# An mLSTM stage taken two chunks at a time, with its 64-channel products in two halves of the array

## The chip, the cores and the metric

The kernel runs on one core of a Trainium2 chip. The metric is the device time of one execution in microseconds; three runs of the kernel before gave 2682.82, 2683.15 and 2689.93 us. The profile is of one more execution. Engines are named as in the profile: PE multiplies matrices (PEld is its weight load), DVE, ACT and POOL work on elements, and SP issues the transfers (DMA).

## What is computed

One layer of a bidirectional encoder, for 2048 tokens of 1024 numbers in float32: a norm, one large projection, a gated delta rule (GDN) in 8 heads, an mLSTM in 8 heads, an output projection, a norm and a residual. The change concerns the mLSTM alone. For one head and one direction it is, with C and n carried from chunk to chunk:

```python
m_t = jnp.maximum(b_c + m_state[..., None], mi_c)
inter = jnp.exp(b_c + m_state[..., None] - m_t)
w_intra = jnp.exp(lw_c - m_t[..., None]) * qk_c
num = inter[..., None] * jnp.einsum('bhld,bhde->bhle', q_c, c_state) + jnp.einsum('bhts,bhse->bhte', w_intra, v_c)
den = inter * jnp.einsum('bhld,bhd->bhl', q_c, n_state) + jnp.sum(w_intra, axis=-1)
h = num / jnp.maximum(jnp.abs(den), jnp.exp(-m_t))[..., None]
c_state = carry_dec[..., None, None] * c_state + jnp.einsum('bhld,bhle->bhde', wk, v_c)
```

q and k have 64 channels a head, v has 128. Both directions' h are added, normed over the head, and multiplied by two gates. The kernel works with chunks of 128 tokens, 16 a head, and appends a column of ones to v, so that den is column 128 of num.

## The kernel before

**Stages.** Norm, projection of gates, q, k, v of the GDN (to some 827 us of the span); then the rest of the projection beside the inversion of the GDN's triangular matrices, in which the mLSTM's q, k and v are made, convolved and stored to DRAM (827 to 1400 us: functions `m_k`, `m_q`, `m_v`, and `merges`); then the GDN's scan over chunks (1400 to 2063 us); then the mLSTM's chunks, with the first half of the output projection woven in as filling (2063 to 2476 us); then the rest of the output projection.

**The mLSTM stage.** Head by head, 16 chunks each, from the last chunk to the first. For each chunk `weights` makes scores k·q with one product over 128 rows (L1336; rows 64 to 127 of the weights are zeros that POOL set once, since there are only 64 channels), two exponentials on ACT (L1339) and one product on DVE (L1344: W). `core` then adds two products per direction in PSUM: scaled q times the state (L1382, the other direction's 64 rows being zeros) and W times v (L1386). DVE makes the denominators (L1389, L1390, L1393), ACT scales the first direction (L1395) and DVE adds the second (L1397), ACT sums the squares (L1402). Both directions' states lie in one tile of 128 rows, direction 0 in rows 0 to 63; `states` makes the sum k v for the next head, one step per chunk, with two accumulating products of 128 columns (L1274, the keys lying beside 64 zero columns), and DVE updates the state (L1282). POOL spreads the keys (L1229), masks the decay rows (L1320) and multiplies the decay by q (L1328: `qe`).

**What sets the order.** PE's and POOL's orders are written out by hand in this stage; `weave` puts 648 matmuls of the output projection (L1183, 128x512) evenly between the steps of `core`, two steps a chunk, 2.57 matmuls a step. DVE, ACT and SP follow an order that a scheduler chose when the kernel was built; every engine works through its own list in that order. In the stage from 827 to 1400 us PE alone is ordered by hand. PSUM in the mLSTM stage: 2 banks for scores, 2 for `pn` (one chunk each), 1 for the states, 1 for transposes, 2 for the filling.

In `m_q` the conv's result is stored to `mkq_d` and released. `load_block` loads scores' operands and decay rows two blocks of 4 chunks ahead.

## Time and profile before

| what | us |
|---|---|
| median of 3 runs | 2683.15 |
| profiled execution, own time | 2685.29 |
| its span, first to last instruction | 2683.6 |
| stage with the inversions and the mLSTM's q, k, v | 827 to 1400 |
| start of the mLSTM stage | 2063 to 2132 |
| mLSTM chunks with states woven in | 2132 to 2428 |
| mLSTM chunks without (the last head) | 2428 to 2470 |

Lines with an L are lines of the kernel before. A matmul in float32 over 128 or 129 columns shows as two records (two passes), one in the filling as one record. Starts of successive matmuls tell how long PE takes for one; the recorded length also holds the time until its last result is out, which overlaps the next.

### The profile page before, as it was taken

The page shows a single profiled execution, that of the slowest core. Times are in us where ns is not written, and L with a number is a line of the kernel's source. Part 1 is how long each engine was busy: PE and PEld are TensorE (multiplying, and loading weights), DVE is VectorE, ACT ScalarE, POOL GpSimd, SP SyncE. Part 2 cuts the span into 40 slices and gives each one's busy share as a digit, 9 for nine tenths or more (in the row PEclk, how much of TensorE's full clock was granted, in tenths as well). Part 3 has the DMA queues.
Part 4 walks back from the last instruction along what each step waited for, and adds up shares of the span by engine and source line. Part 5 has one row for each costly group of instructions (what it writes and reads, how often), then busy time and mean ns, then how long its engine had stood idle before and what let it go on. Part 6 is the DMA issues. An engine that isn't in the chain of part 4 may idle for free.

```text
span 2683.6 us, 49675 instructions
## 1 busy us (share of the span) xinstructions
PE 2575.4 (96%) x16974; PEld 2174.6 (81%) x16974; DVE 1652.3 (62%) x4062; ACT 1220.8 (45%) x3284; POOL 1010.3 (38%) x1497
## 2 busy tenths in 40 slices
PE   7999999999999999999999999999999699999998
PEld 6778877778887877778788888888888599998887
DVE  5547767777777888888625555555554466665333
ACT  6446666666662334344333333333333455555221
POOL 2136655676553333333211121212112455554133
PEclk9999999999999999999999999999998799999999
DMA  4135555565554344444436777667775888875564
GB/s 155 56 91 171 173 154 169 168 181 177 159 171 156 111 150 133 152 146 142 146 121 201 212 218 216 192 197 213 209 215 162 247 241 234 236 215 153 190 197 151
DMA packets 453158, 468.21 MB, mean 174 GB/s; under 512 B 34825, under 2 KB 306089, under 8 KB 452905
## 3 DMA queue, kind: packets, MB, share of 16 engines
q1 hardware_dynamic: 452905, 465.03, 57.9%
q8 instruction: 136, 2.23, 0.3%
q14 instruction: 117, 0.96, 0.1%
HBM read 301.92 MB, written 162.99 MB: 173 GB/s over the span
## 4 chain that ended last, share of the span: by engine, by line
PE 61%; DVE 12%; issue 10%; DMA 9%; POOL 5%; ACT 3%; SPq 1%; POOLq 0%; DVEq 0%; ACTq 0%
PE acc L273 33%; PE po L1183 5%; DVE cacc L586 3%; DMA E<-grow_d 2%; DVE tmp L843 2%; DVE dm L847 2%; PE ps L1017 2%; PE pn L1386 2%; PE pn L1382 2%; PE po L1054 2%; PE ps L1040 2%; PE po L1053 2%; PE ps L1008 2%; DMA wr<-in_w_in_dram 2%; PE pc L1274 2%
## 5 line engine op out<-in xcount | busy, mean ns | idle before, releaser
L273 PE MATMUL acc<-hh,wh 128*128 128x512 f32 x2048 | 832.7, 407 | 0.0
L273 PE MATMUL acc<-hl,wh 128*128 128x512 f32 x2048 | 826.5, 404 | 0.0
L273 PE MATMUL acc<-hh,wl 128*128 128x512 f32 x2048 | 821.7, 401 | 0.0
L273 PEld LDWEIGHTS acc<-hh,wl 128*128 128x128 f32 x2048 | 388.1, 189 | 72.5 <-issue 1.0
L273 PEld LDWEIGHTS acc<-hh,wh 128*128 128x128 f32 x2048 | 388.3, 190 | 69.7 <-issue 1.2
L273 PEld LDWEIGHTS acc<-hl,wh 128*128 128x128 f32 x2048 | 388.5, 190 | 69.1 <-issue 1.0
L231 POOL TENSOR_TENSOR wl<-wr,wh 128x256 fp32r<-128x256 f32 x256 | 205.2, 815 | 605.0 <-ACT wh L230 453.9
L586 DVE SCALAR_TENSOR_TENSOR cacc<-raw,gcw,cacc 128x512 f32<-128x512 f32 x256 | 214.7, 866 | 77.9 <-POOL raw L602 38.8
L1183 PE MATMUL po<-woh,ch 128*128 128x512 f32 x512 | 210.8, 412 | 12.7 <-ACT woh L1159 11.9
L1183 PE MATMUL po<-wol,ch 128*128 128x512 f32 x512 | 207.5, 406 | 2.3 <-POOL wol L1160 2.3
L1183 PE MATMUL po<-woh,cl 128*128 128x512 f32 x512 | 206.5, 404 | 0.0
L151 POOL TENSOR_TENSOR rs<-rs,mhalf 128x4 f32<-128x4 f32 x64 | 64.1, 1008 | 367.0 <-DVE rs L148 222.4
L230 ACT CAST wh<-wr 128x256 fp32r<-128x256 f32 (+1 forms) x260 | 97.8, 403 | 221.6 <-DMA wr<-in_w_in_dram 138.6
L717 POOL COPY dg<-T 32x128 f32<-32x128 f32 x256 | 151.1, 590 | 16.6 <-DVE T L707 6.7
L707 DVE SCALAR_TENSOR_TENSOR T<-pk,sc,E 128x256 f32<-128x256 f32 x256 | 109.7, 474 | 47.4 <-PE pk L704 39.6
L893 POOL COPY Z<-ZD 32x256 f32<-32x256 f32 x128 | 91.7, 717 | 114.3 <-DMA Z<-uq_d 77.9
L586 DVE SCALAR_TENSOR_TENSOR cacc<-raw,mcw,cacc 128x512 f32<-128x512 f32 x128 | 101.0, 807 | 41.2 <-ACT cacc L582 20.8
L586 DVE SCALAR_TENSOR_TENSOR kq<-raw,gcw,kq 128x512 f32<-128x512 f32 x128 | 102.5, 806 | 31.9 <-ACT kq L582 22.1
L1183 PEld LDWEIGHTS po<-woh,ch 128*128 128x128 f32 x512 | 97.5, 191 | 26.9 <-ACT woh L1159 12.6
L1183 PEld LDWEIGHTS po<-wol,ch 128*128 128x128 f32 x512 | 97.4, 190 | 16.8 <-POOL wol L1160 3.8
L1045 DVE SCALAR_TENSOR_TENSOR sn<-sn,eGL,ps 128x128 f32<-128x128 f32 x224 | 67.9, 345 | 69.7 <-PE ps L1040 69.7
L1183 PEld LDWEIGHTS po<-woh,cl 128*128 128x128 f32 x512 | 97.2, 190 | 14.6
(604 smaller groups left out, 4973.2 us busy)
## 6 DMA issues: line engine op xcount, KB each, us to landing
kv<-kv_d SPq DMA_DIRECT2D x256, 256.0 KB, 3.7
wr<-in_w_in_dram SPq DMA_DIRECT2D x256, 128.0 KB, 2.7
uq_d<-T SPq DMA_DIRECT2D x64, 512.0 KB, 4.0
uq<-uq_d SPq DMA_DIRECT2D x256, 128.0 KB, 3.6
zg_d<-zt SPq DMA_DIRECT2D x64, 256.0 KB, 2.7
E<-grow_d SPq DMA_DIRECT2D x64, 256.0 KB, 6.0
kv_d<-tk SPq DMA_DIRECT2D x64, 256.0 KB, 2.5
Z<-uq_d SPq DMA_DIRECT2D x32, 512.0 KB, 4.4
```

The source lines that it names most:

```text
L151: nc.gpsimd.tensor_tensor(out=rs, in0=rs, in1=mhalf[:, :CB], op=ALU.pow)
L230: nc.scalar.copy(out=hi, in_=raw[:, :, :n])
L231: nc.gpsimd.tensor_tensor(out=lo, in0=raw[:, :, :n], in1=hi.bitcast(F32), op=ALU.subtract)
L273: nc.tensor.matmul(ps, l[:, k % KH, :], r[b][:, k, :], start=(k == 0 and i == 0), stop=(k == KC - 1 and i == 2),)
L586: nc.vector.scalar_tensor_tensor(out=acc, in0=raw[:, t : t + TB], scalar=cw[:, t * n_ct + ct : t * n_ct + ct + 1], in1=acc, op0=ALU.mult, ...
L707: nc.vector.scalar_tensor_tensor(out=T2[d][:, :, i], in0=pk, scalar=sc[:, u, c : c + 1], in1=E[d][:, i].unsqueeze(1).broadcast_to([P, 2, P ...
L717: nc.gpsimd.tensor_copy(out=dg[qs, :, at : at + CB], in_=T2[d][qs, 1, :, qs].rearrange("p c i -> p i c"),)
L843: nc.vector.tensor_tensor(out=tv, in0=L[:, j, j + 1 : 32].unsqueeze(2).broadcast_to([P, n, m_]), in1=M[:, j : j + 1, 0:m_].broadcast_to([P ...
L847: nc.vector.tensor_tensor(out=M[:, j + 1 : 32, 0:m_], in0=M[:, j + 1 : 32, 0:m_], in1=tv, op=ALU.subtract,)
L893: nc.gpsimd.tensor_copy(out=self.Z[bs, :, :, bs], in_=ZD[bs].rearrange("p x (d c) -> p d c x", d=2)[:, :, self.qs],)
L1045: nc.vector.scalar_tensor_tensor(out=sn[d], in0=st[d], scalar=eGL[:, u, c : c + 1], in1=ps[d][:, 2], op0=ALU.mult, op1=ALU.add,)
L1183: nc.tensor.matmul(po, l[:, i, :], r[:, ns], start=(first and i == 0 and j == 0), stop=(last and i == H - 1 and j == 2),)
```

## The change

- `m_q` (second stage): for each of 16 blocks of 512 tokens and each direction, two loads of the decay row `in_d`, spread over 64 partitions each, one POOL product over 128x512 with the conv's result, and two stores to new DRAM tiles `mqe_d`. `load_block` then loads the finished `qe` with one transfer; its POOL products (L1328), and the zeros in `qe`, `kq` and `wk` with the copies that spread the keys (L1229), go.
- `core` goes by pairs of chunks, four steps a pair. Both chunks' scores (64 rows each) run in the two row halves of the array, as do the two directions' products of scaled q and state; the states' products run in its two column halves. Number of matmul records is the same for these; W times v stays as it was.
- One PSUM tile `pn` of 4 banks holds a pair's four sums and, beside them, the next pair's scores. There is one such tile (`bufs=1`). The denominators are made for a pair at once. `ps_c` holds two states.

```diff
-            ps_q = st_.enter_context(tc.tile_pool(name="ps_q", bufs=2, space=PSUM, reuse_waits="tile"))
-            ps_n = st_.enter_context(tc.tile_pool(name="ps_n", bufs=2, space=PSUM, reuse_waits="tile"))
+            ps_n = st_.enter_context(tc.tile_pool(name="ps_n", bufs=1, space=PSUM, reuse_waits="tile"))
...
+                for d in range(2):
+                    t = mpool.tile([P, TB], F32, tag="tk", name="qs")
+                    for j in range(2):
+                        nc.sync.dma_start(
+                            out=t[j * 64 : (j + 1) * 64, :],
+                            in_=in_d[d * H + 2 * i + j, bs].partition_broadcast(64),
+                        )
+                    nc.gpsimd.tensor_tensor(out=t, in0=t, in1=so, op=ALU.mult)
+                    for j in range(2):
+                        nc.sync.dma_start(
+                            out=mqe_d[2 * i + j][d * 64 : (d + 1) * 64, bs],
+                            in_=t[j * 64 : (j + 1) * 64, :],
+                        )
...
+                            nc.tensor.matmul(
+                                pc[half(d), e], wks[h, b][:, i, d, :], vs[h, b][:, i, :],
+                                start=True, stop=True,
+                            )
...
+            def scores(pn, h, c):
+
+                kq, i = blk[h, c // CB][0], c % CB // 2
+                for d in range(2):
+                    nc.tensor.matmul(
+                        pn[:, d, 0, VW : VW + P], kq[half(d), i, 0, :], kq[half(d), i, 1, :],
+                        start=True, stop=True,
+                    )
...
+                    qe, pn = blk[h, b][1], pair_tile()
+                    if g + 1 < len(items):
+                        hn, cn = items[g + 1]
+                        scores(pn, hn, cn)
+                    for e in range(2):
+                        ce = c - 1 + e
+                        i = ce % CB
+                        for d, slot in enumerate((ce, NC - 1 - ce)):
+                            nc.tensor.matmul(
+                                pn[:, d, e, :VW], qe[half(d), i * P : (i + 1) * P],
+                                C[half(d), slot, :], start=True, stop=False,
+                            )
...
+                    for e in range(2):
+                        v = vs[h, b][:, (c - 1 + e) % CB, :]
+                        for d in range(2):
+                            nc.tensor.matmul(pn[:, d, e, :VW], W[e][:, d], v, start=False, stop=True)
+                    yield
+                    dn = ms.tile([P, 2, 2], F32, tag="dn", name="dn")
+                    den = pn[:, :, :, P]
...
+                    for e in (1, 0):
...
+                        nc.scalar.activation(
+                            out=oc, in_=pn[:, 0, e, :P], func=AF.Copy, scale=dn[:, 0, e : e + 1]
+                        )
+                        nc.vector.scalar_tensor_tensor(
+                            out=oc, in0=pn[:, 1, e, :P], scalar=dn[:, 1, e : e + 1], in1=oc,
+                            op0=ALU.mult, op1=ALU.add,
+                        )
```

**PE, one chunk in the loop before** (names: `pn` sums, `pq` scores, `pc` states, `pt` transposes of finished blocks, `po` filling):

```order
L1382 MATMUL pn<-C_22810,qe_22802 128x129
L1386 MATMUL pn<-v,W 128x129
L1382 MATMUL pn<-C_22810,qe_22802 128x129
L1386 MATMUL pn<-v,W 128x129
L1183 MATMUL po<-woh_22998,cl 128x512
L1183 MATMUL po<-woh_23008,ch 128x512
L1183 MATMUL po<-wol_23009,ch 128x512
L1336 MATMUL pq<-kq_22794 128x128
L1274 MATMUL pc<-v,wk_22772 128x129
L1274 MATMUL pc<-v,wk_22771 128x129
```

PE, one pair of chunks in the loop now, from the scores of the next pair to the first filling behind W times v:

```order
L1331 MATMUL pn<-kq 128x128 x2
L1381 MATMUL pn<-C_22984,qe 128x129 x4
L1269 MATMUL pc<-v,wk 64x129 x4
L1197 MATMUL po<-woh_23150,ch 128x512
L1197 MATMUL po<-wol_23151,ch 128x512
L1397 MATMUL pn<-v,W 128x129 x4
L1197 MATMUL po<-woh_23150,cl 128x512
```

Six half-array products over rows, four over columns and four full ones stand together, and the next row of L1331 comes behind some 8 fillings; it is the first writer of the one `pn` tile.

**ACT in the loop before** (`o` scales a chunk, `junk` sums its squares, `E` are exponentials):

```order
L1395 ACTIVATE o<-pn,dn 128x128
L1339 ACTIVATE E<-rb,cb 128x128 x2
L1402 ACTIVATE junk,so<-o 128x128
L1395 ACTIVATE o<-pn,dn 128x128
L1339 ACTIVATE E<-rb,cb 128x128 x2
L1402 ACTIVATE junk,so<-o 128x128
```

ACT in the loop now, one pair and a bit (`ch` and `acc` belong to the filling):

```order
L1341 ACTIVATE E<-rb,cb 128x128 x4
L1414 ACTIVATE o<-pn,dn 128x128
L1422 ACTIVATE junk,so<-o 128x128
L1414 ACTIVATE o<-pn,dn 128x128
L1422 ACTIVATE junk,so<-o 128x128
L1341 ACTIVATE E<-rb,cb 128x128 x4
L1414 ACTIVATE o<-pn,dn 128x128
L1185 CAST ch<-ct 128x1024
L1214 COPY acc<-po 128x512
L1422 ACTIVATE junk,so<-o 128x128
```

The exponentials no longer stand between a chunk's `o` and `junk`; the second `o` of a pair stands behind the first `junk`, and in some pairs the filling's `ch` or `acc` stands between them too.

**SP in the second stage now**, at the end of one `m_q` (before, the rows with `qs` were not there):

```order
L783 DMA mqe_d_113<-qs 64x512
L777 DMA qs<-in_d 64x512 x4
L901 DMA Z<-uq_d_69 128x2x512
L213 DMA wr<-in_w_in_dram 128x2x128 x2
L770 DMA mkq_d_107<-cacc 128x4x128 x2
L783 DMA mqe_d_113<-qs 64x512
L783 DMA mqe_d_114<-qs 64x512
L783 DMA mqe_d_113<-qs 64x512
L783 DMA mqe_d_114<-qs 64x512
L777 DMA qs<-in_d 64x512 x4
L960 DMA uq_d_68<-Z 256x1x512
```

A store of `qs` waits for its POOL product, and the loads behind it for the store; the weights' loads (`wr`) and the inversion's (`Z`) stand in the same queue.

## Rows read from the trace of the kernel before

**Rows 1.** The page: engines' busy time, share of the span, instructions.
```profile
PE 2575.4 (96%) x16974; PEld 2174.6 (81%) x16974; DVE 1652.3 (62%) x4062; ACT 1220.8 (45%) x3284; POOL 1010.3 (38%) x1497
```

**Rows 2.** Windows: length, then busy us by engine; clock, DMA share, GB/s.
```profile
core 0: us, PE busy (x) PEld busy (x) DVE busy (x) ACT busy (x) POOL busy (x), PEclk, DMA share, GB/s
827.00:1400.00 573.00, 545.70 (x5646) 438.49 (x5645) 425.10 (x839) 216.94 (x516) 173.35 (x302) 0.98 0.43 137
2063.00:2132.45 69.45, 40.49 (x174) 35.06 (x174) 26.21 (x67) 21.88 (x53) 23.17 (x24) 0.68 0.89 251
2132.45:2435.02 302.57, 302.54 (x2120) 277.42 (x2121) 187.66 (x698) 165.63 (x570) 172.21 (x187) 1.00 0.82 230
```

**Rows 3.** Windows of line L1382 alone, four records a chunk.
```profile
2132.70:2428.00 295.30, 80.19 (x416) 68.81 (x417) 1.00 0.83 232
2428.00:2470.40 42.40, 13.96 (x72) 11.70 (x72) 1.00 0.45 132
```

**Rows 4.** Timeline of one chunk, all engines: start, us, what [idle before].
```profile
2156.09 0.39 PE L1382 MATMUL pn<-C,qe 128*128 128x129 f32 x2
...
2156.32 0.39 PE L1386 MATMUL pn<-v,W 128*128 128x129 f32 x2
...
2156.74 0.16 DVE L1389 TENSOR_TENSOR dn<-pn,em 128x2 f32<-128x2 f32 x1 [0.97 <-PE pn L1386]
...
2157.39 0.37 ACT L1395 ACTIVATE o<-pn,dn 128x128 f32<-128x128 f32 x1 [1.19 <-PE pq L1336]
2157.46 0.40 PE L1183 MATMUL po<-wol,ch 128*128 128x512 f32 x1
...
2157.69 0.39 PE L1183 MATMUL po<-woh,cl 128*128 128x512 f32 x1
...
2157.79 0.35 DVE L1397 SCALAR_TENSOR_TENSOR o<-pn,dn,o 128x128 f32<-128x128 f32 x1 [0.50 <-ACT o L1395]
2157.92 0.60 PE L161 MATMUL pt<-ident,o 128*128 128x128 f32 x4
2158.18 0.31 ACT L1402 ACTIVATE junk<-o 128x128 f32<-128x128 f32 x1 [0.42 <-DVE o L1397]
...
2158.36 0.39 PE L1382 MATMUL pn<-C,qe 128*128 128x129 f32 x2
...
2158.49 0.68 ACT L1339 ACTIVATE E<-rb,cb 128x128 f32<-128x128 f32 x2
```

**Rows 5.** Timeline of PE in the second stage, at products of 64 rows and columns.
```profile
1002.75 0.39 PE L273 MATMUL acc<-hl,wh 128*128 128x512 f32 x1
1002.98 0.39 PE L273 MATMUL acc<-hh,wl 128*128 128x512 f32 x1
1003.29 0.68 PE L877 MATMUL px<-Z,V 64*64 64x64 f32 x16
...
1004.18 0.44 PE L877 MATMUL p__10442<-VV,Z 32*32 32x32 f32 x15
1004.55 0.50 PE L273 MATMUL acc<-hh,wh 128*128 128x512 f32 x1
1004.88 0.39 PE L273 MATMUL acc<-hl,wh 128*128 128x512 f32 x1
```

**Rows 6.** Groups by form, PE, 827 to 1400 us: count, busy, mean ns, idle before.
```profile
L877 PE MATMUL px<-Z,V 64*64 64x64 f32 x512 | 22.2, 227 | 0.0
```

**Rows 7.** Groups by form, 2200 to 2400 us: count, busy, mean ns, idle before.
```profile
L1328 POOL TENSOR_TENSOR qe<-qe,kq 64x512 f32<-64x512 f32 x36 | 48.7, 1352 | 1.4
L1172 DVE TENSOR_TENSOR cl<-ct,ch 128x1024 fp32r<-128x1024 f32 x8 | 10.8, 1353 | 0.3
L1171 ACT CAST ch<-ct 128x1024 fp32r<-128x1024 f32 x8 | 8.3, 1039 | 1.3 <-PE po L1183 1.2
```

**Rows 8.** Transfers: KB each, median us from issue to landing.
```profile
mwk_d<-tk SPq DMA_DIRECT2D x32, 256.0 KB, 2.8
qe<-in_d SPq DMA_DIRECT2D x64, 128.0 KB, 4.3
kq<-mkq_d SPq DMA_DIRECT2D x32, 128.0 KB, 5.4
```

**Rows 9.** Waits from 827 to 1400 us: total, times, longest.
```profile
SPq L212 <- POOL wl L231: 81.0, 42, 7.5
PE pt L611 <- ACT cacc L591: 18.5, 5, 5.6
```

More of the change, by code (lines that the diff above doesn't have):

```diff
@@ L68 @@
     mkq_d = [dram.tile([2, 64, NC, 2, P], F32, name=f"mkq_d{i}") for i in range(H // 2)]
+    mqe_d = [dram.tile([P, S], F32, name=f"mqe_d{h}") for h in range(H)]
     mwk_d = [dram.tile([P, NC, 2, 64], F32, name=f"mwk_d{h}") for h in range(H)]
@@ L1249, with half @@
                 nc.vector.memset(C[:, 0, :], 0.0)
+            def half(d):
+                return slice(d * 64, (d + 1) * 64)
             def states(h):
                 C = Cs[h % 2]
-                if h == 0:
-                    spread_keys(0, outer)
-                    spread_keys(0, inner)
-                for t in range(NC):
+                first = pair_tile() if h == 0 else None
+                for t in range(0, NC, 2):
                     if h > 0 and t == 0:
                         load_values(h, inner)
-                        spread_keys(h, inner)
                     if h + 1 < H and t == NC // 2:
@@ L1305, in load_block @@
                     rb.append(t)
-                qe = qes[j % 3]
-                for d in range(2):
-                    nc.sync.dma_start(
-                        out=qe[d * 64 : (d + 1) * 64, d, :],
-                        in_=in_d[d * H + h, bs].partition_broadcast(64),
-                    )
+                qe = ms.tile([P, TB], F32, tag="qe", name="qe", bufs=3)
+                nc.sync.dma_start(out=qe, in_=mqe_d[h][:, bs])
                 blk[h, b] = (kq, qe, rb)
@@ L1317, in mask_block @@
                     return
-                kq, qe, rb = blk[h, b]
+                rb = blk[h, b][2]
                 for d in range(2):
@@ L1350, in core @@
             def core():
-                items = [(h, NC - 1 - i) for h in range(H) for i in range(NC)]
+                items = [(h, NC - 1 - i) for h in range(H) for i in range(0, NC, 2)]
                 ready = []
@@ L1355, in core @@
                 load_block(1)
-                for i, _ in enumerate(states(0)):
-                    if i % 2:
-                        yield
+                for _ in states(0):
+                    yield
                 mask_block(0)
-                nxt = weights(*items[0])
-                for k, (h, c) in enumerate(items):
+                pn = pair_tile()
+                scores(pn, *items[0])
+                h, c = items[0]
+                nxt = [weights(pn, h, c - 1 + e) for e in range(2)]
+                for g, (h, c) in enumerate(items):
                     C, W, b = Cs[h % 2], nxt, c // CB
@@ L1395, in core @@
-                    nc.scalar.activation(out=oc, in_=pn[:, 0, :P], func=AF.Copy, scale=dn[:, 0:1])
-                    next(following, None)
-                    nc.vector.scalar_tensor_tensor(
-                        out=oc, in0=pn[:, 1, :P], scalar=dn[:, 1:2], in1=oc,
-                        op0=ALU.mult, op1=ALU.add,
-                    )
-                    junk = ms.tile([P, P], F32, tag="junk", name="junk", bufs=1)
-                    nc.scalar.activation(
-                        out=junk, in_=oc, func=AF.Square, accum_out=so[:, i : i + 1]
-                    )
```

133 lines of the change are left out of this document (57 added, 76 removed).

## Prediction

> **What bounds the kernel now.** I read the shares first, then the stages, then one chunk. PE is busy for 96% of the span [rows 1], and in the mLSTM loop for 302.54 of 302.57 us at full clock [rows 2]: there the sum of PE's work is the time, and DVE, ACT and POOL (188, 166 and 172 us busy) lie beside it. The loop's pace: 416 records of L1382, four a chunk, in 295.30 us, so 104 chunks of 2.84 us, or 5.68 us a pair; the last 18 chunks, whose steps hold no states, take 42.40 us, 4.71 us a pair [rows 3]. In the stage's first 69 us PE idles 29 us while transfers move 251 GB/s; in the second stage it idles 27 of 573 us [rows 2].
>
> **One pair on PE, by parts.** A product of 129 columns is two passes; starts of L1382 and L1386 are 0.23 apart [rows 4], so I take 0.22 us a product. A filling takes 0.23 (2157.46 to 2157.69), four transposes 0.44 (2157.92 to 2158.36) [rows 4]. A pair before: 14 products, 3.1 us, 10.3 fillings, 2.36, and a block's transposes every second pair, 0.22 on average: 5.68, as measured. So the price list closes.
>
> **What the halves save.** Scores, q times state, and states are 10 of the 14 products. If two halves run side by side, they take the time of 5: 1.1 us a pair saved, 69 us over 64 pairs. That two run at once is seen for products of 64 rows and 64 columns: 16 passes in 0.68 us [rows 5]; taking off the 0.23 us that one record of this size lasts [rows 6], 0.45 us for 15 starts is 0.03 each, where 64 columns at the loop's rate (0.11 x 64/129) would be 0.055 alone. Those share neither rows nor columns. Halves that share all rows (states) or all columns (scores, q times state) don't occur in this trace; I take the full saving and keep none as the other end.
>
> **What it adds on PE.** Going from full products to halves, the first start is 0.31 behind the last full one instead of 0.23 (1002.98 to 1003.29), and the 15 starts lose some 0.05; going back costs about 0.09 before 1004.55 and 0.10 behind it (0.33 to the next instead of 0.23) [rows 5]. A pair crosses three times: full to row halves, row to column halves, back: 0.14 + 0.14 + 0.19 = 0.47 us. Bounds 0 and 0.6. PE's own work per pair is then 2.0 + 0.47 + 2.36 + 0.22 = 5.05 us.
>
> **The new wait.** There is one `pn` tile. The first product of a pair's first step (the next pair's scores) must wait until DVE's last add of the pair before has read it. Queued behind it on PE is everything: q times state, states, the fillings. Before, two tiles alternated and a chunk's reading had a whole chunk of PE work to hide in. So I add up the ring.
>
> Front, from the release to the last pass of W times v: three side-by-side products 0.67, states 0.45, crossings 0.47, 2.57 fillings 0.59, seven pass starts of W times v at 0.11, 0.78: 2.96 us.
>
> Back, from that last pass to the release, by a chunk in which nothing else stood between [rows 4]: the pass starts at 2156.43 (2156.32 and 0.11), ends 0.28 later, the denominators start at 2156.74, ACT's `o` at 2157.39, DVE's add at 2157.79, `junk` at 2158.18: 1.75 us. For a pair the three denominator steps come once. The second `o` stands behind the first `junk` on ACT, in the order now built: `junk` with its read-out holds ACT 0.31 (2158.18 to 2158.49), `o` 0.37, 0.03 to DVE, add 0.35, 0.04 to PE. Sum 2.85 us. PE has the fillings of three steps, 7.7 x 0.23 = 1.77, and every second pair the transposes, to cover it: 1.9 to 2.3 us with the last pass. The cover falls short by 0.6 to 0.95 us.
>
> Insertions: each 48 fillings, 4.7 pairs, bring one `ch` of 1.04 on ACT and one `cl` of 1.35 us on DVE [rows 7], and in the order built most of them stand inside the ring (`ch` between two `o`, or ahead of the exponentials; `cl` between the denominators or the two adds). Part of each falls into a gap; I take 1.6 of 2.4 us, 0.35 a pair, and 0.06 for the block's product with the gate between the two adds. Bounds 0 and 0.5.
>
> Ring: 2.96 + 2.85 + 0.41 = 6.2 us a pair, above PE's 5.05 and above the old 5.68. 52 pairs with states: +0.52 each, +27 us. Nine without: ring 6.2 less states and a crossing, 5.6, against 4.71: +8 us. Bounds of the two together: crossings and insertions zero -16, all at the upper end +50.
>
> The Trainium skill ("TensorEngine Tiling (Array Packing)", Performance Considerations, PSUM Bottleneck) says that tiling speeds up TensorE but not the emptying of PSUM, which may then become the bottleneck. By PE's 5.05 us alone the loop would gain 35 us, by the emptying it loses 35; the emptying's rows are those above.
>
> **m_q.** It gains 128 transfers and 32 POOL products. POOL's product over 64x512 took 1.35 us [rows 7]; 32 x 1.35 = 43 us, on an engine busy 173 of 573 us. A decay load of 128 KB lands in 4.3 us, a store in about 2.8 [rows 8]. With two `qs` tiles, a block's loads wait for the last block's stores, so a ring of some 4.3 + 2.7 + 2.8 and 8 issues holds each block for 13 us; blocks come every 7 us, the last two of each `m_q` at once. Behind these waits in SP's queue stand `wr` and `Z` loads, and the conv's buffer, two in all, is held longer, so ACT may wait to evacuate the next projection. Three PSUM banks (some 16 us of PE) and a weight column ahead cover most. SP waits for POOL 81 us there already, and PE lost 18.5 us at conv results [rows 9]. I take 2 us for each of 4 `m_q`: +8, bounds 0 and 40.
>
> **What it takes away elsewhere.** POOL's 64 products of `qe`, the key spreading and the masks' neighbours lie beside a full PE: nothing. In the stage's first 69 us, transfers set the pace; 128 KB a block less to load (the doubled `kq` half [rows 8]) for two blocks at 251 GB/s is 1 us, and first states no longer wait for spread keys: -2, bounds -5 and +3.
>
> **Sum.** +35 + 8 - 2 = +41 us. The profiled execution's 2685.29 (span 2683.6 and 1.7 around it) lies 2.1 above the median of the runs; 2683.15 + 41 gives **2724 us**.
>
> **Rivals.** *The fillings cover the emptying* (faster). Against: 2.85 against at most 2.3 us. For: every price in the ring that no row shows, crossings and insertions, could vanish. Then 5.34 a pair: 52 x -0.34 and 9 x +0.19, with m_q free and the start's 2 us, -18: 2665 us; PE alone (5.05) would be the floor, 2654. It decides at a ring of 5.6 us, 0.6 below mine.
>
> *The ring lands on the old pace* (no change): one of crossings and insertions vanishes, 5.75 us, m_q is free: +2 to +8 us, 2675 to 2691; centre 2685.
>
> *The halves don't run side by side* (the change doesn't do what it says): if the states run one after the other, +0.45 a pair, 52 pairs, +23: 2747 us; if the row halves do too, +0.67 for 61 pairs, +41: 2788. For: no row here shows halves that share rows or columns; against: rows 5's pairs. The Trainium skill ("TensorE: Matmul & The Clock Gate", Part 3: Packing small matmuls) says that a weight load overlaps a running matmul only if its row group differs; by that rule the states, which share all rows, would be the serial ones.
>
> *m_q stalls the second stage*: each conv buffer is released a ring (13 us) late, twice in four heads' pairs, and PE's 16 us of PSUM fall short by some 10 each: +40 in place of +8: 2756 us.
>
> **How the numbers follow.** Chances: forecast 0.50 (2692 to 2745), covered 0.12, old pace 0.13, serial halves 0.13 (half of it at 2747), m_q 0.12. A measurement here can tell 0.3%, 8 us, from no change. Faster 0.12, same 0.13, slower 0.75. The range reaches from the old pace's lower end, 2675, to just short of both halves serial, 2785; left out are the covered case and the dearest of the serial ones, 0.18.
>
> **What would show it.** PE busy well below 100% in the loop, its idle time at the scores (L1331) and ended by DVE's add (L1417); 6.2 us from one pair's first product to the next; ACT's `o` ended by DVE. Half products starting in twos within some 0.01 us, with 0.11 between twos, show the halves; 0.09 more at crossings the crossings. `pn` released before PE asks, and PE full, would make the forecast wrong, and so would SP or ACT waits on `qs` above 20 us.

## The result and the profile after

The changed kernel takes 2780.02 us (median of four runs, 2769.63 to 2783.64) against 2684.05 us: ratio 1.0347, 95% interval 1.0314 to 1.0379. The forecast was 2724 us, so the sign is right and the loss is more than twice as large. The profiled execution took 2782.27 us with a span of 2780.5. Lines with an L are now lines of the changed kernel: scores L1331, q times state L1381, states L1269, W times v L1397, fillings L1197; on ACT the exponentials L1341, `o` L1414, `junk` L1422, `ch` L1185, `acc` L1214; on DVE W L1346, denominators L1401, L1404, L1407, the adds L1417, `cl` L1186; POOL's masks L1316.

The two spans differ by 96.9 us. First records of a line divide it:

| stretch | before | after | difference |
|---|---|---|---|
| up to the scan's first product of w and uq | 1412.4 | 1437.9 | +25.5 |
| from there to the first states' product | 650.5 | 655.8 | +5.3 |
| start of the mLSTM stage, to its sixth pair | 81.2 | 75.4 | -5.8 |
| 50 pairs from there | 284.0 | 340.8 | +56.8 |
| the rest of the mLSTM pairs | 42.1 | 56.0 | +13.9 |
| the rest | 213.4 | 214.7 | +1.3 |

Shares first, against [rows 1]: PE has lost three points, with the same number of instructions.

```profile
PE 2584.2 (93%) x16974; PEld 2130.2 (77%) x16974; DVE 1645.6 (59%) x3870; ACT 1217.9 (44%) x3284; POOL 949.2 (34%) x1420
```

Windows of the changed kernel, in the columns of [rows 2]: second stage, 50 pairs.

```profile
827.00:1437.50 610.50, 569.71 (x5695) 456.38 (x5694) 442.76 (x842) 221.11 (x523) 222.68 (x335) 0.95 0.52 161
2169.00:2509.70 340.70, 279.21 (x1990) 221.57 (x1990) 158.67 (x505) 153.34 (x533) 80.69 (x100) 0.93 0.60 182
```

In the 50 pairs PE is busy for 279 of 341 us and its mean clock is 0.93, where it was full at 1.00. The same stretch by groups of PE (count, busy, mean ns, idle before and what ended it) has all of that idle time at one line:

```profile
L1331 PE MATMUL pn<-kq 64*128 64x128 f32 x200 | 26.1, 333 | 61.1 <-issue 44.6 <-DVE o L1417 16.4
```

So 61 us are waits at the scores, as forecast. They are for the tile, also where the profile names no releaser ("issue"): in 49 of the 50 pairs the scores start 0.10 to 0.15 us behind the end of DVE's second add, in one 0.30. A pair takes 6.82 us on average, where 6.2 was forecast. Here is one with nothing but the ring in the way, 6.02 us, from the timeline:

```profile
2223.90 0.49 PE L1331 MATMUL pn<-kq 64*128 64x128 f32 x4 [1.59 <-issue]
...
2224.77 0.66 PE L1269 MATMUL pc<-v,wk 128*64 128x129 f32 x8
2224.88 0.75 DVE L1346 SCALAR_TENSOR_TENSOR W<-E,pn 128x256 f32<-128x256 f32 x2 [1.08 <-PE pn L1381]
...
2226.16 1.05 PE L1397 MATMUL pn<-v,W 128*128 128x129 f32 x8
...
2227.25 0.16 DVE L1401 TENSOR_TENSOR dn<-pn,em 128x4 f32<-128x4 f32 x1 [0.97 <-PE pn L1397]
...
2227.91 0.37 ACT L1414 ACTIVATE o<-pn,dn 128x128 f32<-128x128 f32 x1 [1.30 <-DVE dn L1407]
...
2228.32 0.35 DVE L1417 SCALAR_TENSOR_TENSOR o<-pn,dn,o 128x128 f32<-128x128 f32 x1 [0.50 <-ACT o L1414]
...
2228.70 0.31 ACT L1422 ACTIVATE junk<-o 128x128 f32<-128x128 f32 x1 [0.42 <-DVE o L1417]
...
2229.01 0.35 ACT L1414 ACTIVATE o<-pn,dn 128x128 f32<-128x128 f32 x1
2229.43 0.34 DVE L1417 SCALAR_TENSOR_TENSOR o<-pn,dn,o 128x128 f32<-128x128 f32 x1
...
2229.92 0.49 PE L1331 MATMUL pn<-kq 64*128 64x128 f32 x4 [0.67 <-DVE o L1417]
```

This is the ring of the prediction, link by link: the second `o` behind the first `junk`, the next scores 0.15 us behind the end of the second add. Its sum without insertions was put at 5.81 us; eight pairs of this kind take 6.02 to 6.06. Two more take 5.83: they are the last step of a head, with four records of the states in place of eight. The 5.83 us that the expectations below name are theirs.

And here is a pair with insertions, 7.28 us, and the first products of the next one:

```profile
2298.01 0.49 PE L1331 MATMUL pn<-kq 64*128 64x128 f32 x4 [0.67 <-DVE o L1417]
...
2300.46 1.05 ACT L1185 CAST ch<-ct 128x1024 fp32r<-128x1024 f32 x1 [2.16 <-PE po L1197]
...
2301.65 1.39 DVE L1186 TENSOR_TENSOR cl<-ct,ch 128x1024 fp32r<-128x1024 f32 x1
...
2302.01 0.57 ACT L1214 COPY acc<-po 128x512 f32<-128x512 f32 x1
...
2302.48 0.69 ACT L1341 ACTIVATE E<-rb,cb 128x128 f32<-128x128 f32 x2
...
2302.96 0.15 DVE L1404 SCALAR_TENSOR_TENSOR dn<-pn,dn 128x4 f32<-128x4 f32 x1
...
2303.36 0.37 ACT L1414 ACTIVATE o<-pn,dn 128x128 f32<-128x128 f32 x1 [0.19 <-DVE dn L1407]
...
2305.29 0.79 PE L1331 MATMUL pn<-kq 64*128 64x128 f32 x4 [2.35 <-issue]
...
2306.87 1.13 PE L1269 MATMUL pc<-v,wk 128*64 128x129 f32 x8
...
2307.93 0.80 PE L1197 MATMUL po<-woh,ch 128*128 128x512 f32 x1
```

Between W times v and `o` stand `cl` on DVE, between the first and second denominators, and `ch`, `acc` and four exponentials on ACT. DVE's chain with `cl` ends last here: `o` waits 0.19 us for it. In other pairs it is the exponentials that end last. They wait for POOL's mask of the block, and `o` stands behind them, as in the pair that begins at 2188.29, where the denominators are ready at 2191.98:

```profile
2191.89 1.28 ACT L1341 ACTIVATE E<-rb,cb 128x128 f32<-128x128 f32 x4 [3.11 <-POOL rb L1316]
...
2193.08 0.35 ACT L1414 ACTIVATE o<-pn,dn 128x128 f32<-128x128 f32 x1
```

ACT's waits for that mask over the 50 pairs, in the kernel before, then in the changed one:

```profile
ACT E L1339 <- POOL rb L1320: 7.7, 17, 1.2
```

```profile
ACT E L1341 <- POOL rb L1316: 65.3, 21, 3.1
```

Behind the wait of 2.35 us the granted clock is at the lower of its two levels, 1.2 in place of 2.4 GHz (0.50 in the window below), and the next pair's products are longer: scores 0.79 us in place of 0.49, a first filling 0.80 in place of 0.50. Behind the wait of 0.67 us at 2298.01 the clock is 1.00 and they are not longer.

```profile
2305.40:2308.00 2.60, 2.60 (x21) 2.04 (x21) 0.75 (x2) 0.79 (x4) 0.00 (x0) 0.50 0.27 100
```

Counted over the 50 pairs by the starts of their records, with a pair's front from its scores to the last pass of W times v and its back from there to the next scores:

| part | us | a pair |
|---|---|---|
| ring without insertions at full clock: fronts of 2.67 to 3.04, backs of 3.00 | 295.6 | 5.91 |
| ten fronts at the lower clock, 1.2 to 2.4 us longer each | 16.8 | 0.34 |
| backs of the 11 pairs with `ch` and `cl` | 14.3 | 0.29 |
| backs of 18 other pairs with exponentials ahead of an `o` | 11.4 | 0.23 |
| the rest | 2.7 | 0.05 |

### The profile page after: what moved, and what is told of

Its sections match the earlier page's. It is cut to its first block, busy times and chain, and to the rows that moved or that the text cites. A ratio compares the mean times of both kernels' runs of the same rounds, so it can differ in the third digit from the quotient of the medians.

```text
span 2780.5 us, 49294 instructions
## 1 busy us (share of the span) xinstructions
PE 2584.2 (93%) x16974; PEld 2130.2 (77%) x16974; DVE 1645.6 (59%) x3870; ACT 1217.9 (44%) x3284; POOL 949.2 (34%) x1420
## 4 chain that ended last, share of the span: by engine, by line
PE 55%; issue 15%; DVE 11%; DMA 10%; POOL 5%; ACT 3%; SPq 1%; POOLq 0%; DVEq 0%; ACTq 0%
PE acc L274 32%; PE po L1197 3%; DVE cacc L587 3%; DMA wr<-in_w_in_dram 2%; DMA E<-grow_d 2%; PE ps L1031 2%; PE ps L1054 2%; PE po L1068 2%; DVE tmp L857 2%; DVE dm L861 2%; PE po L1067 2%; PE ps L1022 2%; PE pt L612 1%; PE pn L1397 1%; POOL xt L1473 1%
## 5 line engine op out<-in xcount | busy, mean ns | idle before, releaser
L1197 PE MATMUL po<-woh,ch 128*128 128x512 f32 x512 | 212.3, 415 | 6.7 <-ACT woh L1173 5.9
L1197 PE MATMUL po<-wol,ch 128*128 128x512 f32 x512 | 208.8, 409 | 2.3 <-POOL wol L1174 2.3
L1197 PE MATMUL po<-woh,cl 128*128 128x512 f32 x512 | 207.8, 407 | 0.0
L1341 ACT ACTIVATE E<-rb,cb 128x128 f32<-128x128 f32 x256 | 82.5, 391 | 123.6 <-POOL rb L1316 80.4
L1197 PEld LDWEIGHTS po<-woh,ch 128*128 128x128 f32 x512 | 99.3, 194 | 30.2 <-ACT woh L1173 7.4
L1197 PEld LDWEIGHTS po<-wol,ch 128*128 128x128 f32 x512 | 99.7, 195 | 23.1 <-POOL wol L1174 3.4
L1197 PEld LDWEIGHTS po<-woh,cl 128*128 128x128 f32 x512 | 99.0, 193 | 20.7 <-issue 2.9
```

The lines of the kernel that those rows point to most:

```text
L1197: nc.tensor.matmul(po, l[:, i, :], r[:, ns], start=(first and i == 0 and j == 0), stop=(last and i == H - 1 and j == 2),)
L1341: nc.scalar.activation(out=E[:, d], in_=rb[d][:, i, :], func=AF.Exp, bias=cb[:, d * H + h, c : c + 1],)
```

## The experiments

All ratios are to the kernel before, measured on the same chip at the same time. The third column is the length of the 50 pairs (100 chunks where the kernel goes by chunks; in all5, c1 and c2 they begin one pair earlier), the fourth the time of the scan's first product of w and uq; both are of one profiled execution.

| kernel | ratio (interval) | 50 pairs, us | scan begins |
|---|---|---|---|
| before | 1 | 284.0 | 1412.4 |
| changed | 1.0347 (1.0314 to 1.0379) | 340.8 | 1437.9 |
| two_pn | 1.0161 (1.0143 to 1.0180) | 293.3 | 1433.7 |
| early_mask | 1.0214 (1.0187 to 1.0240) | 310.4 | 1434.2 |
| o_first | 1.0159 (1.0137 to 1.0180) | 294.1 | 1430.9 |
| cat_pool | 1.0272 (1.0259 to 1.0286) | 317.4 | 1438.7 |
| shift | 1.0333 (1.0316 to 1.0351) | 339.7 | 1433.7 |
| qe_late | 1.0258 (1.0240 to 1.0276) | 335.4 | 1409.2 |
| no_prod | 1.0357 (1.0336 to 1.0377) | 340.5 | 1444.6 |
| prod_only | 1.0291 (1.0270 to 1.0311) | 334.2 | 1432.1 |
| one_pn | 1.0191 (1.0167 to 1.0216) | 318.6 | 1419.1 |
| states_halves | 1.0042 (1.0027 to 1.0057) | 295.8 | 1413.7 |
| all4 | 1.0108 (1.0093 to 1.0123) | 300.9 | 1412.0 |
| all3b | 1.0111 (1.0083 to 1.0138) | 300.5 | 1413.5 |
| all5 | 1.0088 (1.0061 to 1.0115) | 299.3 | 1416.0 |
| c1 | 1.0075 (1.0061 to 1.0090) | 274.2 | 1438.2 |
| c2 | 1.0097 (1.0081 to 1.0113) | 301.5 | 1412.1 |

**Two tiles (two_pn).**

```diff
-                return ps_n.tile([P, 2, 2, 512], F32, tag="pn", name="pn", bufs=1)
+                return ps_n.tile([P, 2, 512], F32, tag="pn", name="pn", bufs=2)
...
                     for e in range(2):
+                        if e == 1:
+                            q_state(1)
                         v = vs[h, b][:, (c - 1 + e) % CB, :]
```

> The changed kernel with two pair tiles in place of one: a pair's four sums and its scores lie in 2 banks (386 of 512 columns each), so two tiles fit where one stood. Since a bank then holds two sums that must be added up one after the other, q times state of the second chunk moves behind W times v of the first: two crossings more between half-array and full products a pair, some 0.33 us. Everything else is the changed kernel's (2780 us; pairs 6 to 55 take 6.82 us on average, 5.83 where nothing but the ring stands in the way). Theory (the loop is slow because PE waits at the scores for DVE's last add on the single tile, and runs at the lower clock behind the longer of these waits): the wait goes, PE is nearly full at clock 1.00, a pair takes PE's own work, 5.05 + 0.33 = 5.4 us; 61 x 1.4 = 87 us less, about 2693 us. Rival (the chain of denominators, o and adds on DVE and ACT, with exponentials, ch and cl between, is itself the bound, or transfers are): PE still idles at other products, a pair takes 6.3 us or more, 2750 us or more.

The wait for the tile goes, and 47 of the loop's 57 extra us with it. Pairs take 5.25 to 5.7 us where nothing is in the way. The mean is 5.87: PE is busy for 5.68 us a pair (284.23 for 50), 0.3 above the theory's 5.4 and as long as a whole pair took in the kernel before, and something new ends last, 0.18 a pair: PE now waits for W at W times v. With the further way in and out of the halves that two banks force, the halves save PE nothing.

```profile
2167.10:2460.40 293.30, 284.23 (x1991) 213.63 (x1990) 153.22 (x505) 148.78 (x531) 83.90 (x100) 0.98 0.68 211
```

```profile
PE pn L1400 <- DVE W L1346: 9.0, 11, 1.7
```

In the longest of these cases (2225.04) `cl`, 1.23 us, stands ahead of W on DVE. The total, 2727 us, is 34 above the theory's 2693 and 23 below the rival's 2750: the tile's wait is the loop's main loss, but not the whole of what keeps the halves from a gain.

**What stands in the ring (early_mask, o_first, cat_pool).** Three edits each take one thing out of it.

```diff
-                    if g % 2 == 0:
-                        mask_block(g // 2 + 1)
+                    if g % 2 == 1:
+                        mask_block(g // 2 + 2)
...
-                    if g % 2 == 1:
+                    if g % 2 == 0:
                         load_block(g // 2 + 2)
```

> The changed kernel with each block of decay rows loaded and masked one pair earlier, so that POOL masks ahead of the block's rs and product and not behind them. In every second pair of the changed kernel four exponentials on ACT wait for that mask (71.7 us in all, 23 times) and o stands behind them, 0.65 us late. Theory (that is part of the ring's insertions): half of the pairs shorten by 0.65 us, 61 x 0.33 = 20 us, 2760 us. Rival (something else, such as the ACT queue behind the exponentials, takes the place of the wait): 2775 to 2785 us.

```diff
                     for e in (1, 0):
...
+                    for e in (1, 0):
+                        i = (c - 1 + e) % CB
                         nc.vector.scalar_tensor_tensor(
...
+                    for e in (1, 0):
...
+                        i = (c - 1 + e) % CB
                         junk = ms.tile([P, P], F32, tag="junk", name="junk", bufs=1)
```

> The changed kernel with ACT's two scalings o of a pair written ahead of both sums of squares (junk); the single tile stays. Theory (the ring of the single tile sets the pace): from the first add to the end of the second 0.75 us in place of 1.43, so 0.68 a pair less, 61 x 0.68 = 41 us, and fewer waits long enough to bring the lower clock: 2725 to 2745 us. Rival (the ring is not the bound, or what is saved is lost to exponentials and ch that now stand ahead of o): 2765 to 2785 us.

```diff
-            nc.scalar.copy(out=ch, in_=raw)
-            nc.vector.tensor_tensor(out=cl, in0=raw, in1=ch.bitcast(F32), op=ALU.subtract)
+            if early:
+                nc.gpsimd.tensor_copy(out=ch, in_=raw)
+            else:
+                nc.scalar.copy(out=ch, in_=raw)
+            (nc.gpsimd if early else nc.vector).tensor_tensor(
+                out=cl, in0=raw, in1=ch.bitcast(F32), op=ALU.subtract
+            )
...
+            parts = load_cat(cp, 0, 0, True)
```

> The changed kernel with the filling's ch and cl (one of each every 48 fillings, 4.7 pairs) made on POOL, which is three quarters idle there, and not on ACT and DVE, where they stand in the ring. Theory (what the ring of the single tile cannot absorb are these insertions; a pair without any takes 5.83 us, the mean is 6.82): pairs of 7.3 to 8.8 us become rare, 0.3 to 0.5 us a pair less, 20 to 30 us, 2750 to 2762 us. Rival (POOL's ch and cl delay its masks, and the exponentials behind them, by as much): 2770 us or more.

Each gains, early_mask and o_first more than the shortened chain alone. The windows of the same 50 pairs of early_mask, then of o_first, say why:

```profile
2160.50:2470.90 310.40, 262.97 (x1990) 207.99 (x1990) 157.50 (x506) 155.68 (x533) 80.69 (x100) 0.99 0.65 200
```

```profile
2161.20:2455.30 294.10, 262.75 (x1990) 206.26 (x1990) 152.73 (x505) 152.62 (x533) 80.70 (x100) 0.99 0.68 211
```

The same 1990 products keep PE busy for 263 us at clock 0.99 in place of 279 at 0.93: once the waits are shorter, 16 us of slow products, 0.33 us a pair, are gone too. Of early_mask's 30 us in the loop, 16 are that, and the other 14 are what the mask had held up: no back holds up an `o` behind exponentials that wait for it any more. cat_pool has 264.00 us at 0.99 as well, and 23 us less loop. Each of the three edits shortened another part of the back, and most of the slow products went with it. The clock's share is read from these rows; no run changes the clock alone.

**Fillings behind W times v (shift).**

```diff
                     next(following, None)
-                    yield
...
                             nc.tensor.matmul(pn[:, d, e, :VW], W[e][:, d], v, start=False, stop=True)
-                    yield
+                    yield 2
```

> The changed kernel with one thing moved: the fillings that stood between the states and W times v (two or three a pair, 0.23 us each) stand behind W times v, where PE waits for the tile. Theory (the ring of the single tile sets the pace): it loses these fillings, 0.6 us a pair, 61 x 0.6 = 37 us, and some of the stretches at the lower clock that follow the longer waits: 2720 to 2740 us, 6.2 us a pair or a little under. Rival (PE's total work or the other engines set the pace): moving work within a pair changes nothing, 2775 to 2785 us.

The loop stays at 339.7 us, as the rival has it, but not for the rival's reason. Counted as above, the fronts take 143.8 us in place of 162.6, and the backs 195.9 in place of 178.2: the theory's gain is there, and the back loses it again. The fillings that were moved now stand ahead of the transposes on PE, and DVE's `zt`, which takes them up, stands ahead of the second add:

```profile
2181.79 0.35 ACT L1413 ACTIVATE o<-pn,dn 128x128 f32<-128x128 f32 x1
...
2182.32 0.69 DVE L164 TENSOR_TENSOR zt<-zt,pt 128x512 f32<-128x512 f32 x1 [0.88 <-PE pt L162]
...
2182.93 0.34 DVE L1416 SCALAR_TENSOR_TENSOR o<-pn,dn,o 128x128 f32<-128x128 f32 x1
```

The second add could have started behind this `o`, at 2182.2; such backs take 3.7 us in place of 3.0. The front, too, gains less than the 0.6 us of the fillings, 0.25 at full clock, since it has a second chain. PE's weight load for W times v waits for DVE:

```profile
PEld pn L1396 <- DVE W L1346: 28.6, 50, 1.4
```

It is not the W that this product uses, which was made a pair earlier, but the one for the next pair: its scores lie in the banks of the same tile, and in the built program W times v waits until DVE has read them. So from the first score to W times v no less than 1.8 us pass (1.0 until DVE starts, 0.75 for both W), where the changed kernel took 2.0 to 2.3 at full clock. The Trainium skill ("PSUM — Partial Sum Buffer", PSUM bank collisions raise a hardware error) says why such an order is kept: TensorE and VectorE must not access one bank of the same partitions at the same time, at different addresses either. The waits of the trace agree; what a collision would do no run here shows.

**The single tile in the kernel before (one_pn).**

```diff
-            ps_n = st_.enter_context(tc.tile_pool(name="ps_n", bufs=2, space=PSUM, reuse_waits="tile"))
+            ps_n = st_.enter_context(tc.tile_pool(name="ps_n", bufs=1, space=PSUM, reuse_waits="tile"))
```

> The kernel before with one part of the change alone: one pn tile (a chunk's) in place of two. The scores keep their own two tiles. Theory (a single tile costs only because in the changed kernel the next pair's scores, its q times state and the states all stand behind it, and a pair is emptied at once): here a chunk's two products with q, two with W take 0.9 us, emptying 1.75 us from the last pass, 2.64 together, below the chunk's 2.84 us, and some five fillings, the scores and the states (1.9 us) stand between: the loop of 104 chunks stays at 295 to 306 us, the total within 12 us of the kernel before. Rival (a single tile alone is what costs): 3.2 us a chunk or more, 330 us, total 40 us more.

The rival's number holds. The window of the 104 chunks, by the records of q times state, against [rows 3]:

```profile
2141.90:2472.20 330.30, 87.37 (x416) 63.12 (x417) 0.99 0.75 207
```

Eleven chunks take 4.0 to 5.2 us, where with two tiles none takes more than 3.4; ten of them are chunks into which a `ch` or `cl` falls. They make some 17 of the 35 us. The other 93 take 3.03 us on average, where a chunk took 2.84 with two tiles. So the ring without insertions is nearly covered, but not quite as worked out, and about half of what the second copy had taken up is the irregular work.

**What the halves save (states_halves).**

```diff
-                                pc, wk_of(h, b)[:, i].rearrange("p s k -> p (s k)")[:, d * 64 : d * 64 + P],
-                                vs[h, b][:, i, :], start=(d == 0), stop=(d == 1),
+                                pc[d * 64 : (d + 1) * 64], wk_of(h, b)[:, i, 2 * d, :],
+                                vs[h, b][:, i, :], start=True, stop=True,
```

> The kernel before with one part of the change alone: each of the two states' products of a chunk writes 64 columns of the array (its own direction's half) in place of 128 with zeros beside them; everything else is the kernel before's. PE is full there, so the loop (416 records of q times state in 295.30 us) shows the price directly. Theory (two column halves run side by side, 0.22 us a chunk saved, and a crossing into and out of half-array products costs some 0.1 us each): from -0.03 to +0.05 us a chunk, the loop 292 to 300 us, total within 8 us of the kernel before. Rival (the halves run one after the other, at the same crossings): +0.2 us a chunk, the loop 316 us, total some 22 us more. Rival (crossings are free): -0.22 us a chunk, the loop 272 us, total 25 us less.

PE stays full at clock 1.00, and 104 chunks take 12.3 us more, 0.12 us a chunk, between the theory's 300 us and the 316 of the first rival:

```profile
2136.50:2444.10 307.60, 80.17 (x416) 68.72 (x417) 1.00 0.80 222
```

PE's timeline of one chunk in this kernel, and of the same place in the kernel before:

```profile
2300.84 0.38 PE L1336 MATMUL pq<-kq 128*128 128x128 f32 x2
2301.15 0.44 PE L1274 MATMUL pc<-v,wk 128*64 128x129 f32 x4
2301.53 0.50 PE L1183 MATMUL po<-woh,cl 128*128 128x512 f32 x1
2301.86 0.39 PE L1183 MATMUL po<-woh,ch 128*128 128x512 f32 x1
```

```profile
2301.52 0.38 PE L1336 MATMUL pq<-kq 128*128 128x128 f32 x2
2301.74 0.61 PE L1274 MATMUL pc<-v,wk 128*128 128x129 f32 x4
2302.10 0.48 PE L1183 MATMUL po<-woh,cl 128*128 128x512 f32 x1
2302.42 0.40 PE L1183 MATMUL po<-woh,ch 128*128 128x512 f32 x1
```

From scores to states 0.31 us in place of 0.22, from the first states' record to the first filling 0.38 in place of 0.36 although half as many starts follow one another. The two halves of a pass start 0.007 us apart, so they do run side by side; but with the 0.22 us that they save, a way in and out of half-array products costs some 0.12 + 0.22 = 0.34 us. That is the 0.14 + 0.19 = 0.33 that the prediction had read from [rows 5], for halves that it had not seen; the 0.1 for each crossing in this run's theory was too low. The Trainium skill ("TensorE: Matmul & The Clock Gate", Part 3: Packing small matmuls) has a weight load overlap a running matmul only where the row groups differ; read so, these halves, sharing all rows, would go one after the other. The trace does not agree: the weight loads of two halves start 0.006 us apart.

**The second stage (qe_late, no_prod, prod_only).** qe_late takes the loads, the product and the stores out of `m_q` and lets `mask_block` make the product from two loads of the decay and two of q:

```diff
+                nc.gpsimd.tensor_tensor(out=qe, in0=qe, in1=q2, op=ALU.mult)
```

> The changed kernel with one part undone: scaled queries are again made in the mLSTM stage (per block two loads of the decay rows, two of q, one POOL product over 128x512 right behind the masks), and m_q does no loads, products and stores for them. Theory (in the second stage the conv's buffer is held by the late loads and the POOL product, ACT waits to evacuate the next projection, PE behind it: 25.5 us from the first products there to the scan's first, and some of the 5 us in the scan): the second stage takes 585 us again in place of 611, total 2750 to 2757 us; the loop's pace stays 6.8 us a pair. Rival (the second stage is slow for another reason, or POOL's product delays the masks in the loop by as much): 2770 us or more.

```profile
827.00:1408.50 581.50, 552.44 (x5687) 443.50 (x5687) 424.96 (x842) 220.85 (x523) 173.70 (x303) 0.98 0.43 139
```

The stage is as short as before, and the loop 5 us shorter, so the 25.5 us are `m_q`'s. How exact that is, the table's last column tells: the eight kernels with the old second stage come to the scan at 1409.2 to 1419.1 us, the seven with the new one at 1430.9 to 1438.7, 22 us later on average. About half of the 25.5 is PE's clock: as many products keep PE busy for 569.71 us at 0.95 (above), in the kernel before for 557.53 at 0.98.

```profile
827.00:1412.00 585.00, 557.53 (x5701) 448.19 (x5700) 426.44 (x842) 220.75 (x523) 174.82 (x304) 0.98 0.44 139
```

In the changed kernel the chain that the prediction named is there (waits of ACT and POOL, then of SP, in the second stage):

```profile
ACT vt L801 <- POOL qs L781: 29.4, 5, 9.0
...
POOL qs L781 <- DMA qs<-in_d: 24.3, 10, 7.0
```

```profile
SPq L783 <- POOL qs L781: 16.2, 15, 2.6
SPq L777 <- DMA mqe_d<-qs: 15.5, 13, 3.3
```

Two kernels keep one half each: no_prod leaves out the line `nc.gpsimd.tensor_tensor(out=t, in0=t, in1=so, op=ALU.mult)`, prod_only the loads and stores around it.

> The changed kernel without POOL's product in m_q: the decay rows are loaded and stored as they are (so the scaled queries lack q). All 128 extra transfers stay. Theory (POOL's product holds the conv's buffer until its loads have landed, ACT waits for that buffer to evacuate the next projection): the second stage loses most of its extra 25 us, 586 to 593 us in place of 611. Rival (the transfers in SP's queue delay weights or the inversion): 603 us or more.

> The changed kernel with the POOL product in m_q on the conv's result alone: its loads of decay rows and its stores are left out, and the mLSTM stage loads the plain decay rows (so the scaled queries lack q). Theory (what holds the buffer is mostly that the loads come late, 24.3 us of POOL's waiting): the second stage takes 586 to 596 us. Rival (POOL's own queue and the 1.35 us of a product hold the buffer): 600 to 611 us.

Neither gives the time back: 1444.6 and 1432.1, so both theories are wrong and both rivals hold. Each half alone does most of the harm or more, and the two don't add. So it is not just the buffer held for late loads. Part of prod_only's loss is seen on DVE, in the groups of the second stage: the inversion's products, 248 of a line, in the kernel before, then in the changed one.

```profile
L843 DVE TENSOR_TENSOR tmp<-dl,dm 128x31 f32<-128x31 f32 (+15 forms) x248 | 99.1, 399 | 7.1
...
L847 DVE TENSOR_TENSOR dm<-dm,tmp 128x31 f32<-128x31 f32 (+15 forms) x248 | 98.3, 396 | 7.2
```

```profile
L857 DVE TENSOR_TENSOR tmp<-dl,dm 128x31 f32<-128x31 f32 (+15 forms) x248 | 109.2, 440 | 7.1
...
L861 DVE TENSOR_TENSOR dm<-dm,tmp 128x31 f32<-128x31 f32 (+15 forms) x248 | 102.0, 411 | 7.2
```

They take 420 and 423 ns in prod_only, and 404 and 395 in no_prod. So POOL's 32 products lengthen DVE's by some 14 us in all. In no_prod the trace points to the queue: SP waits 30.0 us for the decay loads that a store follows at once, with the weights' loads behind it; no run has the transfers without that wait. How the two come to less together than one by one is open.

**All of it together (all4, all3b, all5, c1, c2).** all4 joins qe_late, o_first, early_mask and shift; all3b leaves shift out, loads the first two blocks as the changed kernel does, and has three buffers for the loaded q; all5 also puts the states ahead of the scores:

```diff
+                    next(following, None)
                     qe, pn = blk[h, b][1], pair_tile()
...
-                    next(following, None)
                     yield
```

> The changed kernel with four edits together: scaled queries made in the mLSTM stage again, both scalings o ahead of the sums of squares, masks and their loads a pair earlier, and all fillings behind W times v. Theory: back of the ring some 2.3 us from the last pass of W times v, against 2.4 to 2.6 us of fillings and transposes: the wait nearly vanishes, a pair takes 5.1 to 5.4 us, the second stage 585 us: 2655 to 2675 us, faster than the kernel before (2682). Rival (the three savings overlap, or a DVE or ACT queue with cl and ch takes over): 5.6 us a pair or more, 2685 us or more.

> The changed kernel with three edits: scaled queries made in the mLSTM stage again, both scalings o ahead of the sums of squares, masks and their loads a pair earlier (from the third block on, and with three buffers for the loaded q). Fillings stand where the changed kernel has them. Theory: second stage 582 to 586 us, a pair 5.5 us in place of 6.7: 2670 to 2690 us, level with the kernel before or a little faster. Rival (as with the four edits together, loads arrive late and the stage's start is longer): 2700 us or more.

> The kernel with three edits, and the states' products of a pair put ahead of the scores of the next pair, so that they run while PE would wait for the tile. Theory (whatever need not wait for the tile and stands in front of the first product that does shortens the ring; the products of states and their crossing are 0.65 us): 5.2 to 5.4 us a pair, some 10 to 18 us below the kernel with three edits: 2655 to 2675 us. Rival (W times v then waits for DVE's W, which stands 1.8 us behind the scores whatever lies between): no more than 5 us below it.

All three land near 2715 us, above what the theory gave. Undisturbed pairs do take what was expected (all3b: 5.2 to 5.55), but in all3b four of the 50 take 10.6 to 12.5 us: PE stands at the states and waits for `v` (16.0 us, five times), whose loads stand in SP's queue with the longer loads of qe_late, and the stage's start is some 16 us longer than in the changed kernel in all4 and all3b. all5 gains 5 us on all3b, what the rival allowed. c1 keeps the changed kernel's `m_q`, and takes o_first, early_mask (from the third block on), cat_pool and the states ahead of the scores. c2 is the same with qe_late's `m_q` and each mask ahead of the last block's `rs`.

> The changed kernel, m_q as it is, with all that shortens the ring: ch and cl on POOL, both scalings o ahead of the sums of squares, masks and their loads a pair earlier (from the third block on), states ahead of the scores. Theory: every insertion is out of the ring, PE's own work is the pace, 5.2 to 5.4 us a pair: the mLSTM stage 385 to 395 us in place of 472, the second stage as in the changed kernel (611): 2690 to 2705 us. Rival (another wait comes up at the same place): 2715 us or more.

> All that shortens the ring, and scaled queries made in the mLSTM stage again: ch and cl on POOL, both scalings o ahead of the sums of squares, each block's mask ahead of the last block's rs on POOL (loads where the changed kernel has them), states ahead of the scores, m_q without its loads, products and stores. Theory: second stage 585 us, 5.3 to 5.5 us a pair: 2665 to 2682 us, faster than the kernel before (2690 in the last comparison). Rival (POOL with ch, cl, masks and the product of qe becomes the late one, or loads do): 2690 us or more.

```profile
2167.10:2441.30 274.20, 269.38 (x1995) 200.67 (x1991) 143.43 (x495) 145.37 (x523) 117.80 (x122) 1.00 0.76 227
```

```profile
L1336 PE MATMUL pn<-kq 64*128 64x128 f32 x200 | 24.6, 321 | 0.8 <-ACT junk L1430 0.5
```

c1 settles the loop: with the single tile still there, PE waits 0.8 us at the scores in place of 61.1, its clock is 1.00, a pair takes 5.48 us, and the whole mLSTM stage 400 us against 407 before and 472. The total, 2708 us against 2688 for the kernel before in the same comparison, is what remains of the second stage's 25 us; it is 3 us above the theory's range. In c2 that is gone, but the late loads of `v` are back (17.3 us, five times; c1, without the loads of qe_late, has none), and the rival holds. No kernel beat the one before.

## Why the prediction was right or wrong

**The wait and its place: right.** One tile, PE idle at the scores (L1331), ended by DVE's last add; halves side by side; PE below full. The ring without insertions takes 5.91 us for 5.81, the front 2.91 for 2.96 and the back 3.00 for 2.85, so a part of that closeness is two errors that cancel. The second chain of the front, through DVE's W, was not in the sum; it lies 0.25 us below the front and did no harm here. The covered case and the old pace are out, and so are serial halves.

**The step that failed in the loop: two terms that the ring's sum put at nothing.** The forecast of 6.2 us a pair is 5.81 and insertions of 0.41; measured is 6.82. Of the missing 0.6, 0.34 is PE's clock: the sum prices every product at full clock, though PE was to wait at each pair's scores, and ten fronts ran at the lower level. Another 0.23 are the exponentials. They no longer stand between a chunk's `o` and `junk`, and the sum has no term for them; but they stand ahead of the first `o`, and in 21 of the 50 pairs they wait for a mask that POOL makes behind the last block's `rs` and product. `ch` and `cl`, put at 0.35, cost 0.29; there the prediction was right that a part falls into gaps. All insertions together are 0.57, above the bound of 0.5. The 50 pairs lost 57 us, where 0.52 a pair would be 26; the pairs behind them 14 for 8.

**PE's own work: too low, without effect here.** 5.05 us a pair was the sum; c1, with PE nearly full, takes 5.39 of PE's time (269.38 us for 50 pairs). The crossings are not what was missed: by states_halves a way in and out costs 0.34, for 0.33 read. What makes up the rest was not split by a run. So a covered ring would have ended near c1's pace, 0.2 us a pair below the old one, and not the 0.34 of the covered rival or the 0.63 of its floor.

**The step that failed in the second stage: the cover of `m_q`.** Mechanism right, size wrong: +8 was taken, 2 us for each `m_q`; it cost 25.5, within the bounds of 0 and 40. The cover of three PSUM banks did not carry: ACT's waits for `qs` came to 29.4 us and SP's to 16.2 and 15.5, and waits above 20 us were among the signs that the prediction itself had named for being wrong. POOL's effect on DVE was not on the list, nor was PE's clock, which is half of the 25.5. Of the 56 us by which the result lies above the forecast, `m_q` makes 17, the clock in the 50 pairs 17 and the exponentials 11.

**The start:** -5.8 us against -2 (bounds -5 and +3); the other kernels with the same loads there take 74.5 to 83.2 us for the same stretch, so most of it may be scatter. **The scan:** 5.3 us more, which no step had. The other kernels that share the changed second stage show 650.9 to 654.9 us for the same stretch, so it may be scatter; it stays open.

## What to carry to other kernels

A buffer's second copy also takes up irregular work, here about half of what it was worth: before giving it up, sum the ring with every instruction that the other engines' queues can put into it, masks on a fourth engine included. When PE waits in a ring, ask of the nearest such waits in the trace whether the products behind them run at the lower clock, and count them so. Moving work off one part of a ring can lengthen another: follow what stands behind it. Half-array products pay only where they save more than a way in and out; here one way cost 0.34 us for the 0.22 that the states' halves saved.

## What the runs showed of the hardware

- PE's wait of 2.35 us at the scores was followed by products at the lower clock level (granted clock 0.50), that of 0.67 us was not (1.00); with the waits shortened (o_first, early_mask) the same 1990 products take 263 us and not 279.
- Entering and leaving half-array products costs 0.34 us per way in and out, for column halves between full products (states_halves: 0.12 us a chunk longer, and 0.22 saved). Two column halves that share all rows start 0.007 us apart.
- POOL's products over 128x512 lengthen DVE's small products from 399 to 440 ns and from 396 to 411 on the mean; without POOL's products (no_prod) they take 404 and 395. The Trainium skill ("SBUF — State Buffer", Who interferes with whom) has DVE and GpSimd share one pair of ports under an exclusive lock; the longer means agree, though no run here shows which instruction was held.
